# A two-layer hybrid block on one core: the 31-tap depthwise convolution as matmuls on four column tiles, and all low halves of the weights on VectorE

## The chip, the core and the metric

The kernel runs on one core of a Trainium2 chip. The metric is device time in microseconds (us) of one execution. The kernel before took 1141.38 us (median of 3 runs, 1138.75 to 1142.35). The names of the engines are those of the profile: PE is TensorE's matmul part and PEld its weight load, DVE is VectorE, ACT is ScalarE, POOL is GpSimd, SP is SyncE, which here only issues transfers. SPq is SP's queue of transfers, ACTq is ACT's.

## What is computed

Two layers, each on 256 tokens of width 1024, all in float32. A layer normalises its input, multiplies it with one wide matrix of 16,400 columns, sends pieces of the product through three branches (differential attention, a conformer convolution, a gated delta rule), gates the three results, adds them and multiplies once more. Cut to the branch that the change touches:

```python
def hybrid_layer(x, ...):
    h = rms_norm(x, norm_w)
    proj = h @ w_in                                   # (256, 16400)
    (aq, ak, av, az, c_glu, cz, dq, dk, dvv, dz, db, da, gate_logits) = jnp.split(proj, ...)
    y_a = diff_attention_branch(aq, ak, av, az, ...)  # 8 heads, ends in @ w_attn_out
    y_c = conformer_conv_branch(c_glu, cz, conv_dw_w, conv_dw_b, conv_ln_w, conv_ln_b, w_conv_out)
    y_d = gated_deltanet_branch(dq, dk, dvv, dz, ...) # 4-tap convs, chunked rule, @ w_dn_out
    g_a, g_c, g_d = jnp.split(jax.nn.sigmoid(gate_logits), 3, axis=-1)
    return x + (g_a * y_a + g_c * y_c + g_d * y_d) @ w_out

def conformer_conv_branch(glu_in, z, dw_w, dw_b, ln_w, ln_b, w_o):
    a, g = jnp.split(glu_in, 2, axis=-1)
    u = a * jax.nn.sigmoid(g)                         # (256, 1024)
    u = causal_depthwise_conv(u, dw_w) + dw_b         # 31 taps, each channel by itself
    u = layer_norm(u, ln_w, ln_b)
    u = jax.nn.silu(u) * jax.nn.silu(z)
    return u @ w_o

def causal_depthwise_conv(x, w):                      # w: (31, 1024); zeros stand before token 0
    return lax.conv_general_dilated(x, w[:, None, :], (1,), [(30, 0)],
                                    feature_group_count=1024, ...)
```

## The kernel before

**Weights.** The matrices of a layer are cut into 36 groups of 512 columns (the list `ORDER`), each group into four chunks of 256 rows by 512 columns: 144 chunks of 512 KB a layer, 288 in all. `load_chunk` (L297) handles one. SP's queue loads it into `w_raw` (L301). ACT rounds it to a format that TensorE takes in one pass, `w_hi` (L308). Then `w_lo = w_raw - w_hi` is made (L309) on DVE or on POOL, as a string of 144 digits says (`POOL`, L50). Each of the three tiles has three buffers: a load waits until an earlier `w_lo` has been made from its buffer, and a `w_hi` or `w_lo` waits until PE is done with an earlier chunk.

**Matmuls.** Activations are also kept as high and low half, so each product takes three matmuls (high by high, high by low, low by high). `group_a` (L360) makes the output with channels on partitions, by matmuls over 256 tokens; `group_b` (L323) with tokens on partitions, by matmuls over 512 columns. Both need some 24 times 256 columns a chunk. All other matmuls (the delta rule, attention, transposes) are plain float32 and run as two passes each; the trace has a record for each pass.

**Order.** PE's order is written out by hand. A layer goes through the steps of `SEQ` (L60): `v`, `k`, `q`, `w`, `a`, `z` each stand for groups of matmuls, `c0` and `c1` for the two halves of the conformer's input (L862), and then through gates and output matrices (`y_phase`, L1095). Between the k-steps of a group, `pump` (L266) runs a piece of a side stream (keys, queries and chunks of the delta rule, attention, the final layer norm), if its due time on a counted clock `clk` has come; each `mm` adds its cost in us to that clock. On the other engines a scheduler sets the order by priorities; `load_chunk` runs 340 ahead.

**The convolution.** `c_groups` leaves `u` as two tiles `c_u` of 128 partitions (channels) by 4 by 256 tokens (L877). The generator `conv_ops` (L887) then makes, for each of 8 channel tiles, one ACT instruction (last tap and bias, L891) and 30 instructions on DVE, `c_acc[sh:] += u[:256-sh] * w[30-sh]` (L894): 480 on DVE in the two layers. `filler` (L290) hands them out with the lowest priority at fourteen places of a layer (`CONV_PLAN`), from the second delta-rule value group to the attention output. `ln_stream` (L1151) reads the result `c_acc` late in the layer.

Of the kernel before, what the change touches and what calls it, by code (L numbers as in the profile page):

```python
# [10 lines left out]
F32 = mybir.dt.float32  # L11
# [47 lines left out]
W_AHEAD = 340  # L59
SEQ = "v0 k0 t0 v1 k1 c0 q0 w0 x0 q1 w1 x1 a0 c1 z0 z1 a1".split()  # L60
CONV_PLAN = {}
CONV_PLAN.update({("in", DV + GW): 36, ("in", AQ): 0, ("in", AK): 12, ("in", CA + GW): 32, ("in", DZ): 32, ("in", DZ + GW): 0, ("in", AQ + GW): 0, ("in", AK + GW): 20, ("dn", 0): 28, ("dn", GW): 8, ("in", AZ): 60, ("in", AZ + GW): 0, ("attn", 0): 12, ("attn", GW): 240})


PC_DW, PC_DB, PC_LW, PC_LB, PC_SC, PC_SUB, PC_DNW = 0, 248, 256, 264, 272, 368, 369
PC_N = 370
PR_AL, PR_DT, PR_LAM = 0, 8, 16
# [23 lines left out]
def kernel(  # L91
# [80 lines left out]
    with tc.issue_after(x_dma[-1].ins):  # L172
# [114 lines left out]
    counter = [0]  # L287
    conv = [None]

    def filler(key, ins):  # L290
        n = CONV_PLAN.get(key, 0)
        if n and ins is not None:
            with tc.high_priority(offset=-LOW), tc.issue_after(ins.ins):
                for _ in range(n):
                    next(conv[0], None)

    def load_chunk(l, g, c):  # L297
# [62 lines left out]
    def group_a(l, key, xs, evac, need=()):  # L360
# [3 lines left out]
        for c, (hi, lo) in enumerate(parts):  # L364
            for kk in range(KC):
# [80 lines left out]
    for l in range(DEPTH):  # L446
# [32 lines left out]
        def params():  # L479
# [382 lines left out]
        def c_groups(s):  # L862
# [19 lines left out]
            group_a(l, ("in", CG + s * GW), H, evac_g)  # L882
            group_a(l, ("in", CA + s * GW), H, evac_u)

        ac = act.tile([P, 8, T], F32, name="c_acc")

        def conv_ops():  # L887
            for ct in range(8):
                u = us[ct // 4][:, ct % 4, :]
                w0 = ct * 31  # L890
                S.activation(out=ac[:, ct, :], in_=u, func=AF.Identity,  # L891
                             scale=dww[:, w0 + 30:w0 + 31], bias=pc[:, PC_DB + ct:PC_DB + ct + 1])
                for sh in range(1, 31):
                    V.scalar_tensor_tensor(out=ac[:, ct, sh:T], in0=u[:, 0:T - sh],  # L894
                                           scalar=dww[:, w0 + 30 - sh:w0 + 31 - sh],
                                           in1=ac[:, ct, sh:T], op0=ALU.mult, op1=ALU.add)
# [435 lines left out]
```

## Time and profile before

| | before |
|---|---|
| median of 3 runs | 1141.38 us (1138.75 to 1142.35) |
| the profiled execution: its span, first to last instruction | 1144.1 us |
| mean granted clock of TensorE | 0.971 |
| busy: PE, DVE, ACT, POOL | 90%, 89%, 48%, 31% of the span |
| instructions in the trace | 17280, of them 6372 matmul passes |
| moved by DMA | 158.97 MB, mean 139 GB/s |

The profiled execution has no time of its own beside its span; the span is 2.7 us (0.2%) above the median of the runs. Busy shares of PE count from the start of a matmul to its modelled end, and neighbours overlap, so a PE that is busy isn't a PE at its peak. A row of a group of instructions gives their line in the kernel, the engine, the operation, what it writes and reads, how many there are, their busy time and mean duration, and how long the engine was idle before them and for whom. Windows are stretches of the span, in us from its start; an `x` and a number behind a busy time count instructions. The second layer repeats the first from about 558 us on.

### The profile page before, as it was taken

What the parts mean: (1) busy time and instruction counts of PE and PEld (TensorE: products, weight loads), DVE (VectorE), ACT (ScalarE), POOL (GpSimd) and SP (SyncE); (2) the same over time, 40 slices, a digit from 0 to 9 for tenths busy, and PEclk for the clock granted to TensorE, in tenths of its full rate; (3) what the DMA queues carried; (4) which work ended last, traced back from release to release, by engine and by line L of the source; (5) the groups of instructions that cost most, each with busy time, mean ns of one, the idle gap of its engine ahead of it and who ended that gap; (6) DMA issues with size and microseconds to landing.
All of it is one profiled execution on the core that took longest, in us unless ns stands there. A gap on an engine that the chain in (4) does not pass through costs nothing.

```text
span 1144.1 us, 17280 instructions
## 1 busy us (share of the span) xinstructions
PE 1034.5 (90%) x6372; PEld 901.7 (79%) x6372; DVE 1020.7 (89%) x1996; ACT 547.5 (48%) x995; POOL 359.0 (31%) x168
## 2 busy tenths in 40 slices
PE   7998989899998998898999889889999799899897
PEld 6897988897876876796889889879887678678775
DVE  5879898999998999988577989899999989998966
ACT  5734544344545553345466445443535455434543
POOL 2244132221162125425413332222113412253441
PEclk9999999999998999999999999998999899999998
DMA  6443333233344554454665433332433455545553
GB/s 211 149 127 111 129 125 115 93 111 96 109 129 140 160 178 139 153 173 149 189 208 164 129 116 125 120 102 93 129 111 111 129 157 173 150 152 163 158 172 109
DMA packets 46052, 158.97 MB, mean 139 GB/s; under 512 B 5392, under 2 KB 6416, under 8 KB 45968
## 3 DMA queue, kind: packets, MB, share of 16 engines
q1 hardware_dynamic: 42624, 153.11, 42.2%
q10 hardware_dynamic: 3312, 4.76, 1.3%
q8 instruction: 50, 0.82, 0.3%
q14 instruction: 34, 0.28, 0.1%
q0 software_dynamic: 32, 0.00, 0.1%
HBM read 155.75 MB, written 2.10 MB: 138 GB/s over the span
## 4 chain that ended last, share of the span: by engine, by line
DVE 51%; PE 34%; issue 7%; ACT 3%; DMA 2%; POOL 2%; SPq 0%; ACTq 0%; POOLq 0%; DVEq 0%
PE acc L245 26%; DVE c_acc L894 15%; DVE w_lo L309 10%; PE sg L245 4%; DVE wc L611 4%; DVE dn_t L702 2%; DMA w_raw<-in_wts 2%; ACT w_hi L308 2%; PE sg L249 1%; PE sa L249 1%; ACT a_pe L968 1%; DVE big L1065 1%; POOL w_lo L309 1%; DVE c_acc L1186 1%; PE sa L245 1%
## 5 line engine op out<-in xcount | busy, mean ns | idle before, releaser
L308 ACT CAST w_hi<-w_raw 128x1024 fp32r<-128x1024 f32 (+1 forms) x289 | 301.3, 1044 | 318.7 <-PE acc L245 186.0
L309 POOL TENSOR_TENSOR w_lo<-w_raw,w_hi 128x1024 fp32r<-128x1024 f32 x96 | 251.6, 2622 | 604.1 <-ACT w_hi L308 534.1
L309 DVE TENSOR_TENSOR w_lo<-w_raw,w_hi 128x1024 fp32r<-128x1024 f32 (+1 forms) x193 | 251.9, 1307 | 46.0 <-ACT w_hi L308 45.5
L894 DVE SCALAR_TENSOR_TENSOR c_acc<-c_u,pc,c_acc 128x245 f32<-128x245 f32 (+18 forms) x480 | 275.1, 608 | 2.3
L245 PE MATMUL acc<-h_hi,w_lo 128*128 128x256 f32 x768 | 222.1, 289 | 11.2 <-DVE w_lo L309 8.7
L245 PE MATMUL acc<-h_hi,w_hi 128*128 128x256 f32 x768 | 232.2, 302 | 0.0
L245 PE MATMUL acc<-w_lo,h_hi 128*128 128x512 f32 x512 | 204.5, 399 | 20.6 <-DVE w_lo L309 15.1
L245 PE MATMUL acc<-h_lo,w_hi 128*128 128x256 f32 x768 | 221.4, 288 | 0.0
L245 PE MATMUL acc<-w_hi,h_hi 128*128 128x512 f32 x512 | 212.4, 415 | 1.3 <-ACT w_hi L308 1.3
L245 PE MATMUL acc<-w_hi,h_lo 128*128 128x512 f32 x512 | 203.2, 397 | 0.0
L245 PEld LDWEIGHTS acc<-h_hi,w_lo 128*128 128x128 f32 x768 | 151.3, 197 | 12.4 <-DVE w_lo L309 9.5
L245 PEld LDWEIGHTS acc<-h_lo,w_hi 128*128 128x128 f32 x768 | 151.9, 198 | 0.7
L245 PEld LDWEIGHTS acc<-h_hi,w_hi 128*128 128x128 f32 x768 | 151.7, 198 | 0.5
L245 PEld LDWEIGHTS acc<-w_lo,h_hi 128*128 128x128 f32 x512 | 98.0, 191 | 44.3 <-DVE w_lo L309 20.9
L245 PEld LDWEIGHTS acc<-w_hi,h_lo 128*128 128x128 f32 x512 | 97.6, 191 | 20.9
L245 PEld LDWEIGHTS acc<-w_hi,h_hi 128*128 128x128 f32 x512 | 98.2, 192 | 18.8 <-ACT w_hi L308 2.1
L245 PE MATMUL acc<-w_lo,y_hi 128*128 128x512 f32 x192 | 77.5, 404 | 5.8 <-DVE w_lo L309 4.8
L611 DVE SCALAR_TENSOR_TENSOR wc<-wc,pc 128x255 f32<-128x255 f32 (+2 forms) x144 | 82.4, 608 | 0.3
L245 PE MATMUL acc<-w_hi,y_hi 128*128 128x512 f32 x192 | 78.2, 407 | 0.0
L245 PE MATMUL acc<-w_hi,y_lo 128*128 128x512 f32 x192 | 76.7, 399 | 0.1
L245 PEld LDWEIGHTS acc<-w_lo,y_hi 128*128 128x128 f32 x192 | 37.1, 193 | 17.2 <-DVE w_lo L309 7.9
L926 POOL TENSOR_TENSOR wa<-wa 128x512 f32<-128x512 f32 x16 | 23.7, 1478 | 70.4 <-DVE wa L924 64.3
(298 smaller groups left out, 1504.5 us busy)
## 6 DMA issues: line engine op xcount, KB each, us to landing
w_raw<-in_wts SPq DMA_DIRECT2D x288, 512.0 KB, 3.5
big<-in_x SPq DMA_DIRECT2D x4, 256.0 KB, 5.0
big<-in_x ACTq DMA_DIRECT2D x4, 256.0 KB, 4.6
x_keep<-big ACTq DMA_DIRECT2D x4, 256.0 KB, 4.3
vv<-in_fnw ACTq DMA_DIRECT2D x1, 512.0 KB, 4.9
big<-x_keep SPq DMA_DIRECT2D x2, 256.0 KB, 6.1
big<-x_keep ACTq DMA_DIRECT2D x2, 256.0 KB, 4.9
out<-c_u ACTq DMA_DIRECT2D x2, 256.0 KB, 2.0
```

The costliest lines, as they stand in the source:

```text
L245: TE.matmul(**kw)
L249: TE.transpose(out=out, in_=in_, identity=ident[0:n, 0:n])
L308: S.copy(out=hi[:, kk], in_=raw[:, kk])
L309: eng.tensor_sub(out=lo[:, kk], in0=raw[:, kk], in1=hi[:, kk].bitcast(F32))
L611: V.scalar_tensor_tensor(out=cv[:, i, s:T], in0=cs[:, i, 0:T - s], scalar=wts_[i][:, 3 - s:4 - s], in1=cv[:, i, s:T], op0=ALU.mult, op1=AL ...
L702: V.tensor_tensor(out=t1[:, :, 0:i + 1], in0=z[:, :, 0:i + 1], in1=nrep[:, 0:i + 1, :, i].rearrange("p j c -> p c j"), op=ALU.mult)
L894: V.scalar_tensor_tensor(out=ac[:, ct, sh:T], in0=u[:, 0:T - sh], scalar=dww[:, w0 + 30 - sh:w0 + 31 - sh], in1=ac[:, ct, sh:T], op0=ALU.m ...
L926: G.tensor_tensor(out=ra, in0=ra, in1=rb, op=ALU.add)
L968: S.activation(out=pe[:, m, :], in_=scs[m][:, ii, :], func=AF.Exp, bias=nmxs[m][:, ii:ii + 1], accum_out=sums[:, m:m + 1])
L1065: V.scalar_tensor_tensor(out=os_[:, h, :], in0=os_[:, h, :], scalar=rv[:, t, h:h + 1], in1=tzs[t][:, h, :], op0=ALU.mult, op1=ALU.mult)
L1186: V.tensor_scalar(out=pz[:, f, :], in0=pz[:, f, :], scalar1=ln4[:, ct:ct + 1], scalar2=ln4[:, 8 + ct:9 + ct], op0=ALU.mult, op1=ALU.add)
```

## The change

The convolution moves to PE. Its 31 taps, with a zero tap added, are cut into 8 groups `q` of 4. A tile `u4` holds, on its four blocks of 32 partitions, the same 32 channels at shifts 0, 1, 2 and 3 tokens; a tile `wd` holds diagonal 32x32 blocks of tap weights, one for each shift, channel block and `q`. One matmul of 128 rows by 32 columns adds four taps for 32 channels; four of them, one for each block `j` of 32 channels, go to the four blocks of 32 output partitions, and eight `q` finish 128 channels. `conv_group` has two such channel tiles, runs four times a layer (`d0`, `d1`, `d2` in `SEQ`, and once after the gates of the delta rule), and ACT takes the result from PSUM with bias and scale. That is 512 matmuls in plain float32 in the two layers.

`u4` needs `u` in another layout, so `c_groups` writes `u` to DRAM (`u_keep`, SP's queue), and `conv_load` reads it back in four transfers of 32 partitions, behind a load of 1 MB of `wd`. `u4` and `wd` have one buffer each. The `filler` and its plan are gone. The string `POOL` is all zeros: all 288 `w_lo` are made on DVE. A small load of positions moves from POOL's queue to ACT's.

```diff
-POOL = ("000001001001001000011010010001001001100101001001000110001010001010001101"
-        "101001001000100001001010001001001001001001010001001001001001001001001000")
+POOL = "0" * 144
-SEQ = "v0 k0 t0 v1 k1 c0 q0 w0 x0 q1 w1 x1 a0 c1 z0 z1 a1".split()
-CONV_PLAN = {}
-CONV_PLAN.update({("in", DV + GW): 36, ...})
+SEQ = "v0 k0 t0 v1 k1 c0 q0 w0 d0 x0 q1 w1 d1 x1 a0 c1 z0 z1 d2 a1".split()
+TAPQ = 8
+    u_keep = dram.tile([D, T], F32, name="u_keep")
+    u4 = const.tile([P, 8, T], F32, name="u4")
+    wd = const.tile([P, 2, TAPQ, 4, 32], F32, name="wd")
+        for i in range(1, 4):
+            G.memset(u4[32 * i:32 * i + 32, :, 0:i], 0.0)
-        nc.gpsimd.dma_start(out=pos_i, in_=positions.rearrange("b (c p) -> p (b c)", p=P))
+        nc.scalar.dma_start(out=pos_i, in_=positions.rearrange("b (c p) -> p (b c)", p=P))
...
             group_a(l, ("in", CG + s * GW), H, evac_g)
             group_a(l, ("in", CA + s * GW), H, evac_u)
+            nc.sync.dma_start(out=u_keep[s * GW:(s + 1) * GW].rearrange("(a p) t -> p a t", p=P), in_=us[s])
+            conv_load(2 * s)
 
         ac = act.tile([P, 8, T], F32, name="c_acc")
 
-        def conv_ops():
-            for ct in range(8):
-                u = us[ct // 4][:, ct % 4, :]
-                w0 = ct * 31
-                S.activation(out=ac[:, ct, :], in_=u, func=AF.Identity,
-                             scale=dww[:, w0 + 30:w0 + 31], bias=pc[:, PC_DB + ct:PC_DB + ct + 1])
-                for sh in range(1, 31):
-                    V.scalar_tensor_tensor(out=ac[:, ct, sh:T], in0=u[:, 0:T - sh],
-                                           scalar=dww[:, w0 + 30 - sh:w0 + 31 - sh],
-                                           in1=ac[:, ct, sh:T], op0=ALU.mult, op1=ALU.add)
-                    yield
+        def conv_load(n):
+            with tc.high_priority(offset=W_AHEAD):
+                nc.sync.dma_start(out=wd.rearrange("p f q j c -> p (f q j c)"), in_=cwd[l, n])
+                for i in range(4):
+                    nc.sync.dma_start(
+                        out=u4[32 * i:32 * i + 32, :, i:T],
+                        in_=u_keep[n * 2 * P:(n + 1) * 2 * P, 0:T - i].rearrange("(g c) t -> c g t", c=32))
+
+        def conv_group(n):
+            ps = acc_tile().rearrange("p (f t) -> p f t", f=2)
+            for f in range(2):
+                ct = 2 * n + f
+                for q in range(TAPQ):
+                    for j in range(4):
+                        mm((T - 4 * q) / 2400.0, out=ps[32 * j:32 * j + 32, f, 4 * q:T], lhsT=wd[:, f, q, j, :],
+                           rhs=u4[:, 4 * f + j, 0:T - 4 * q], start=(q == 0), stop=(q == TAPQ - 1))
+                S.activation(out=ac[:, ct, :], in_=ps[:, f, :], func=AF.Identity, scale=0.5,
+                             bias=pc[:, PC_DB + ct:PC_DB + ct + 1])
+                pump()
+            if n in (0, 2):
+                conv_load(n + 1)
...
         steps = {..., "d": conv_group}
...
         y_phase(GATE_D, "dn", (yd, list(enumerate(s_z))))
+        conv_group(3)
```

What the change does to the order shows at three places. The first is PE behind the step `w0` of the first layer (the first delta-rule value group, `group_a`; `t` is a tile of the delta rule's keys, transposed here). Before, the transposes are followed by further weight matmuls:

```order
L245 MATMUL acc<-h_lo,w_hi 128x256
L245 MATMUL acc<-h_hi,w_lo 128x256
L249 MATMUL sg<-cst,t_1251 128x128 x4
L245 MATMUL acc<-h_hi,w_hi 128x256
L245 MATMUL acc<-h_lo,w_hi 128x256
```

Now, with the step `d0` there (shown as `u_80` and `wd`; x4 are the four column tiles):

```order
L249 MATMUL acc<-h_lo,w_hi 128x256
L249 MATMUL acc<-h_hi,w_lo 128x256
L253 MATMUL sg<-cst,t_1256 128x128 x4
L249 MATMUL acc<-u_80,wd 32x256 x4
L249 MATMUL acc<-u_80,wd 32x252 x4
L249 MATMUL acc<-u_80,wd 32x248 x4
L249 MATMUL acc<-u_80,wd 32x244 x4
L249 MATMUL acc<-u_80,wd 32x240 x4
L249 MATMUL acc<-u_80,wd 32x236 x4
L249 MATMUL acc<-u_80,wd 32x232 x4
L249 MATMUL acc<-u_80,wd 32x228 x4
L249 MATMUL sg<-ones,gx 128x1 x8
```

Eight rows of four are one channel tile; one side stream's step stands between the two tiles of a group, and no weight matmul.

The second is DVE some way into the delta rule's first chunk (`gx` and `dn_r` are its tiles, L799 to L818; L920 and L924 are attention's rotary step). Before, runs of the convolution stand between the side streams and the `w_lo`:

```order
L818 TENSOR_TENSOR gx<-sg,dec 128x512
L309 TENSOR_TENSOR w_lo<-w_raw,w_hi 128x1024
L920 TENSOR_TENSOR wa<-acc,cosr 128x512
L924 TENSOR_TENSOR wa<-acc,sinr 128x8x32 x2
L894 SCALAR_TENSOR_TENSOR c_acc<-c_u,pc,c_acc 128x254 x2
L894 SCALAR_TENSOR_TENSOR c_acc<-c_u,pc,c_acc 128x253 x2
L894 SCALAR_TENSOR_TENSOR c_acc<-c_u,pc,c_acc 128x252 x2
L894 SCALAR_TENSOR_TENSOR c_acc<-c_u,pc,c_acc 128x251 x2
```

Now the same stretch has the `w_lo` and the side streams alone:

```order
L811 TENSOR_TENSOR gx<-sg,dec 128x512
L304 TENSOR_TENSOR w_lo<-w_raw,w_hi 128x1024
L923 TENSOR_TENSOR wa<-acc,cosr 128x512
L927 TENSOR_TENSOR wa<-acc,sinr 128x8x32 x2
L923 TENSOR_TENSOR wa<-acc,cosr 128x512
L792 SCALAR_TENSOR_TENSOR dn_r_2187<-sg,neg_eg,dn_r_2187 128x128 x4
L304 TENSOR_TENSOR w_lo<-w_raw,w_hi 128x1024
```

The convolution is gone from between them, and a `w_lo` comes after fewer other instructions.

The third is SP's queue from the start of the kernel. Before, it held the input and 85 chunks in a row; now:

```order
L884 DMA wd<-in_cwd 128x2048
L159 DMA big<-in_x 128x512 x2
L296 DMA w_raw<-in_wts 128x1024 x29
L877 DMA u_keep<-c_u 128x4x256
L296 DMA w_raw<-in_wts 128x1024
L886 DMA u_80<-u_keep 32x8x256
L886 DMA u_80<-u_keep 32x8x255
L886 DMA u_80<-u_keep 32x8x254
L886 DMA u_80<-u_keep 32x8x253
L296 DMA w_raw<-in_wts 128x1024 x8
L884 DMA wd<-in_cwd 128x2048
```

The first 1 MB of `wd` stands ahead of the input. The write of `u_keep` waits for DVE's last instruction on `u` (L877 of the kernel before), the first read of `u_keep` for the landing of that write, and the second `wd` for PE's last matmul of `d0`; the chunks stand behind each of these.

More of the change, by code (lines that the diff above doesn't have):

```diff
@@ L59 @@
 W_AHEAD = 340
-SEQ = "v0 k0 t0 v1 k1 c0 q0 w0 x0 q1 w1 x1 a0 c1 z0 z1 a1".split()
-CONV_PLAN = {}
-CONV_PLAN.update({("in", DV + GW): 36, ("in", AQ): 0, ("in", AK): 12, ("in", CA + GW): 32, ("in", DZ): 32, ("in", DZ + GW): 0, ("in", AQ + GW): 0, ("in", AK + GW): 20, ("dn", 0): 28, ("dn", GW): 8, ("in", AZ): 60, ("in", AZ + GW): 0, ("attn", 0): 12, ("attn", GW): 240})
-PC_DW, PC_DB, PC_LW, PC_LB, PC_SC, PC_SUB, PC_DNW = 0, 248, 256, 264, 272, 368, 369
-PC_N = 370
+SEQ = "v0 k0 t0 v1 k1 c0 q0 w0 d0 x0 q1 w1 d1 x1 a0 c1 z0 z1 d2 a1".split()
+TAPQ = 8
+PC_DB, PC_LW, PC_LB, PC_SC, PC_SUB, PC_DNW = 0, 8, 16, 24, 120, 121
+PC_N = 122
 PR_AL, PR_DT, PR_LAM = 0, 8, 16
@@ L97 @@
     wba: bass.AP,
+    cwd: bass.AP,
     pch: bass.AP,
@@ L287 @@
     counter = [0]
[L288 to L295, printed above, removed]
     def load_chunk(l, g, c):
@@ L332, in group_b @@
             if k == KT - 1:
-                filler(key, evac(ps))
+                evac(ps)
             pump()
@@ L382, in group_a @@
                 if k == KT - 1:
-                    filler(key, evac(ps))
+                    evac(ps)
                 pump()
@@ L459 @@
         scw = pc[:, PC_SC:PC_SC + 96]
-        dww = pc[:, PC_DW:PC_DW + 248]
         ln2 = lay.tile([P, 16], F32, name="ln2")
@@ L484, in params @@
                 masks()
-            V.tensor_scalar(out=dww, in0=dww, scalar1=0.5, scalar2=None, op0=ALU.mult)
             V.tensor_scalar(out=ln2, in0=pc[:, PC_LW:PC_LW + 16], scalar1=0.5, scalar2=None, op0=ALU.mult)
@@ L883, in c_groups @@
             group_a(l, ("in", CA + s * GW), H, evac_u)
+            nc.sync.dma_start(out=u_keep[s * GW:(s + 1) * GW].rearrange("(a p) t -> p a t", p=P), in_=us[s])
+            conv_load(2 * s)
         ac = act.tile([P, 8, T], F32, name="c_acc")
-        def conv_ops():
-            for ct in range(8):
-                u = us[ct // 4][:, ct % 4, :]
-                w0 = ct * 31
-                S.activation(out=ac[:, ct, :], in_=u, func=AF.Identity,
-                             scale=dww[:, w0 + 30:w0 + 31], bias=pc[:, PC_DB + ct:PC_DB + ct + 1])
-                for sh in range(1, 31):
-                    V.scalar_tensor_tensor(out=ac[:, ct, sh:T], in0=u[:, 0:T - sh],
-                                           scalar=dww[:, w0 + 30 - sh:w0 + 31 - sh],
-                                           in1=ac[:, ct, sh:T], op0=ALU.mult, op1=ALU.add)
-                    yield
-        conv[0] = conv_ops()
+        def conv_load(n):
[18 more added lines that the diff above has]
+                conv_load(n + 1)
         def q_group(hs):
@@ L1084 @@
         steps = {"v": v_group, "k": k_group, "c": c_groups, "q": q_group, "w": dv_group, "x": x_start,
-                 "a": qk_groups, "z": dz_group, "t": tables}
+                 "a": qk_groups, "z": dz_group, "t": tables, "d": conv_group}
         for step in SEQ:
@@ L1307 @@
     pch = np.concatenate(
-        [chan(a["conv_dw_w"], 8), chan(a["conv_dw_b"], 8), chan(a["conv_ln_w"], 8),
+        [chan(a["conv_dw_b"], 8), chan(a["conv_ln_w"], 8),
          chan(a["conv_ln_b"], 8), chan(a["dn_conv_w"], 24),
          chan(a["attn_subln_w"], 1), chan(a["dn_norm_w"], 1)], axis=2)
+    taps = np.zeros((DEPTH, 4 * TAPQ, D), np.float32)
+    taps[:, :31] = a["conv_dw_w"][:, ::-1]
+    taps = taps.reshape(DEPTH, TAPQ, 4, 4, 2, 4, 32)
+    cwd = np.zeros((DEPTH, 4, 4, 32, 2, TAPQ, 4, 32), np.float32)
+    for c in range(32):
+        cwd[:, :, :, c, :, :, :, c] = taps[..., c].transpose(0, 3, 2, 4, 1, 5)
+    cwd = cwd.reshape(DEPTH, 4, P, 2 * TAPQ * 4 * 32)
     prow = np.concatenate(
@@ L1316 @@
     arrays = {
-        "x": a["x"].reshape(T, D), "positions": a["positions"], "wts": wts, "wba": wba,
+        "x": a["x"].reshape(T, D), "positions": a["positions"], "wts": wts, "wba": wba, "cwd": cwd,
         "pch": pch, "prow": prow,
@@ L1320 @@
     }
-    nc = _bacc.Bacc("TRN2", target_bir_lowering=False, num_devices=1)
+    nc = _bacc.Bacc("TRN2", target_bir_lowering=False, num_devices=1, dynamic_dma_scratch_size=1024)
     aps, feed = [], {}
```

## Prediction

> **What bounds the kernel now.** I read the page first, then stretches of the span by stage, then the paces of PE's matmuls, then the groups on DVE and POOL.
>
> The page, busy shares and the chain of waits that ended last:
>
> ```profile
> span 1144.1 us, 17280 instructions
> PE 1034.5 (90%) x6372; PEld 901.7 (79%) x6372; DVE 1020.7 (89%) x1996; ACT 547.5 (48%) x995; POOL 359.0 (31%) x168
> ...
> DVE 51%; PE 34%; issue 7%; ACT 3%; DMA 2%; POOL 2%; SPq 0%; ACTq 0%; POOLq 0%; DVEq 0%
> PE acc L245 26%; DVE c_acc L894 15%; DVE w_lo L309 10%; PE sg L245 4%; DVE wc L611 4%; DVE dn_t L702 2%; DMA w_raw<-in_wts 2%; ACT w_hi L308 2%; PE sg L249 1%; PE sa L249 1%; ACT a_pe L968 1%; DVE big L1065 1%; POOL w_lo L309 1%; DVE c_acc L1186 1%; PE sa L245 1%
> ```
>
> PE and DVE are both near 90%, and the chain runs over DVE more than over PE; the convolution (L894) alone is 15% of it. So taking work from DVE can pay, but only down to what PE needs by itself. How much is that? First the stages: the two layers before the convolution starts (25 to 195, 583 to 754), while it runs (195 to 480, 754 to 1040), and after it.
>
> ```profile
> core 0: us, PE busy (x) PEld busy (x) DVE busy (x) ACT busy (x) POOL busy (x), PEclk, DMA share, GB/s
> 0.00:25.00 25.00, 17.77 (x68) 13.88 (x69) 13.36 (x27) 13.71 (x26) 4.94 (x7) 1.00 0.66 215
> 25.00:195.00 170.00, 152.48 (x1218) 145.60 (x1218) 147.81 (x329) 84.29 (x140) 53.32 (x27) 0.96 0.40 128
> 195.00:480.00 285.00, 258.66 (x1408) 215.33 (x1407) 275.32 (x555) 129.87 (x275) 83.24 (x35) 0.96 0.41 128
> 480.00:583.00 103.00, 97.64 (x524) 83.30 (x524) 79.67 (x94) 53.34 (x72) 40.06 (x19) 0.99 0.57 182
> 583.00:754.00 171.00, 157.96 (x1258) 150.34 (x1257) 148.22 (x325) 86.12 (x142) 53.33 (x27) 0.98 0.43 136
> 754.00:1040.00 286.00, 259.67 (x1428) 217.07 (x1427) 276.62 (x560) 131.00 (x276) 83.75 (x35) 0.97 0.41 131
> 1040.00:1144.10 104.10, 90.29 (x479) 76.17 (x477) 79.66 (x111) 49.22 (x67) 40.34 (x19) 0.97 0.47 152
> ```
>
> While the convolution runs, DVE is busy 275 of 285 us and PE idles 26 a layer; before that, DVE is busy 148 of 170 without any convolution. The granted clock is below 1 in the same stretches: 4% of 170 us is 7 us lost, 4% of 285 is 11. Idle time and lost clock together make 41 us in the two early stages (17.5, 13.0, 6.8, 3.4), 73 in the two middle ones (26.3, 26.3, 11.4, 8.6), 12 late (without the tail) and 2.5 at the start.
>
> Those are lower bounds, since a PE in a gap counts as busy to the modelled end of its last matmul. So I also go by PE's paces, from the chain and the timeline (start, length, what, how many):
>
> ```profile
> 1040.73 17.16 PE acc L245 x143
> ...
> 180.60 1.39 PE acc L245 x6
> ...
> 4.70 0.47 PE L249 MATMUL sa<-cst,big 128*128 128x128 f32 x1 [4.70 <-DMA cst<-in_consts]
> ...
> 367.53 1.05 PE L245 MATMUL sg<-big,a_at 128*128 128x128 f32 x8
> 368.34 0.47 PE L245 MATMUL acc<-w_hi,y_hi 128*128 128x512 f32 x1
> ...
> 1135.21 0.39 PE L245 MATMUL acc<-w_hi,c_acc 128*128 128x512 f32 x1
> ```
>
> Unhindered, a 256-column matmul of the weight groups takes 17.16/143 = 0.120 us, a 512-column one 1.39/6 = 0.232, a float32 pass of 128 columns (368.34 - 367.53)/8 = 0.10. A chunk is 24 of the first kind (96 chunks) or 12 of the second (192): 276 + 535 = 811 us. The other 6372 - 4608 = 1764 passes would be 178 us at 0.10; some are much shorter, and I take 150. So PE needs 961 us, and 183 are lost, 4.7 before its first matmul and 8.5 after its last. The 170 between are 1.33 times the 128 above; split in the same ratio: **early 54, middle 97, late 16, start 3**.
>
> **What goes from DVE.**
>
> ```profile
> L309 POOL TENSOR_TENSOR w_lo<-w_raw,w_hi 128x1024 fp32r<-128x1024 f32 x96 | 251.6, 2622 | 604.1 <-ACT w_hi L308 534.1
> L894 DVE SCALAR_TENSOR_TENSOR c_acc<-c_u,pc,c_acc 128x245 f32<-128x245 f32 (+18 forms) x480 | 275.1, 608 | 2.3
> ...
> L309 DVE TENSOR_TENSOR w_lo<-w_raw,w_hi x193: 685/1217/3743, 9.3 to 1128.6; 128x1024 fp32r<-128x1024 f32 x191, 128x512 fp32r<-128x512 f32 x2
> ...
> L894 DVE SCALAR_TENSOR_TENSOR c_acc<-c_u,pc,c_acc x480: 431/461/2656, 196.5 to 1037.8; 128x249 f32<-128x249 f32 x14, 128x246 f32<-128x246 f32 x10, 128x243 f32<-128x243 f32 x10, 128x237 f32<-128x237 f32 x10
> ```
>
> (The last two rows give minimum, median and maximum in ns.) The convolution leaves 275.1 us. The 96 `w_lo` from POOL come in at the median of 1.217 us: 117. DVE is then busy 1020.7 - 275.1 + 117 = 863 us, 75% of the old span. It should be less: the convolution's instructions have a median of 461 ns, a mean of 608 and a maximum of 2656, about the length of one `w_lo` on POOL (2622). I read that as DVE standing still while POOL's instruction runs. If so, a `w_lo` on POOL cost DVE about what it costs to make it there, and the early stages, which have POOL's `w_lo` and no convolution, lose nothing by the swap. `w_lo` also comes 1.4 us sooner after `w_hi`.
>
> In the middle stage POOL is busy 83 us, 252/359 of it by `w_lo`: 22 of them at 2.622. DVE falls there from 275 to 275 - 138 + 27 = 164 of 285 us: 58%. I take 70 of the 97 lost there as won. Early, DVE is at 87% and stays near it; what helps is that `d0` and `d1`, PE work without new `w_lo`, stand in that stage and let DVE catch up. I take 24 of 54. Late, the layer norm's chain on DVE stays: 4 of 16. **Won: 98.** Between ends: 40, if most gaps are chains of dependent steps that a freer DVE doesn't shorten, and 130.
>
> **What comes to PE.** 512 float32 matmuls, two passes each, of 256 down to 228 columns, 242 in the mean. A pass over the whole array, and passes on two row halves (attention's scores, L951, four matmuls with the halves alternating):
>
> ```profile
> 502.73 0.59 PE L245 MATMUL sa<-gx,ones 128*128 128x256 f32 x2
> ...
> L245 PE MATMUL sa<-gx,ones x8: 377/377/378, 483.6 to 1059.5; 128*128 128x256 f32 x8
> ...
> 358.88 1.13 PE L245 MATMUL sa<-t,t 64*128 64x256 f32 x8
> 359.95 0.39 PE L245 MATMUL sa<-mask_at,identb 128*128 128x256 bf16 x2
> ...
> 358.90:359.18 0.28, 0.28 (x2) 0.28 (x4) 0.00 (x0) 0.00 (x0) 1.00 0.83 337
> ```
>
> On the whole array the second pass starts 0.59 - 0.377 = 0.213 us after the first, so 242 columns take 0.201. On row halves, eight passes took 359.95 - 358.88 = 1.07 us, not 8 x 0.213 = 1.70, and in the first 0.28 us two were on their way. So tiles of the array do run at once: four slots of 0.213 and 0.22 for getting in and out. Column tiles don't occur in this trace. Bounds: 1024 x 0.201 = 206 us one after another, a fourth of it, 52, if four run at once; the nearest row, the row halves, reached its full factor, so I take 52. Sixteen stretches with 0.22 each add 3: **55**. The upper end is 209. ACT's part is the same as before (16 instructions for 16).
>
> [...]
>
> **What comes to the queues.**
>
> ```profile
> SPq L301 <- DVE w_lo L309: 431.2, 135, 7.7
> SPq L301 <- POOL w_lo L309: 361.6, 93, 8.4
> ...
> w_raw<-in_wts SPq DMA_DIRECT2D x288, 512.0 KB, 3.5
> ...
> x_keep<-big ACTq DMA_DIRECT2D x4, 256.0 KB, 4.3
> ...
> 6.25 0.90 PE L249 MATMUL sa<-cst,big 128*128 128x128 f32 x3 [1.08 <-DMA big<-in_x]
> ```
>
> At the start, 1.05 MB of `wd` stand ahead of the input that PE waits for at 6.25. At the 215 GB/s of the first window that is 4.9 us, at its full share (215/0.66) 3.2: **4**. Each layer has two round trips of `u` through DRAM: the write lands after some 4.3 us, then 1 MB of `u4` takes 3.2 to 4.9, and chunks stand behind both. Cover: SP waits for free buffers 431 + 362 us in all, so loads are early; up to five chunks (14 us of PE) lie ahead. Without that cover a trip costs 9 us; four cost 0 to 36, and I take **4**. The waits of `wd` for PE's `d0` hold chunks only while PE runs `d0` itself. In all, 8 x (1.05 + 1.04) + 2.1 = 19 MB are added to 159, no bound.
>
> **Sum**, on the profiled execution: 1144 - 98 + 55 + 4 + 4 = 1109. The median of the runs is 0.2% below that span, so **1106 us** for the runs.
>
> **Rivals** (times of the span, less 3 for the runs).
> - *Only two passes run at once* (0.13): a tile's second pass goes before the next tile's first, or its weight load lies open, so the gain is a half. The convolution is 103 + 3; more PE work also fills gaps, so won 106: 1144 - 106 + 106 + 8 = 1152, **1149**. For it: the eight passes on row halves would also take 1.07 us as five slots in strict order. Against: two at once from the first slot.
> - *No overlap* (0.08): 209, won 115: 1144 - 115 + 209 + 8 = 1246, **1243**. For it: no row shows column tiles. Against: nothing but the row halves.
> - *The gaps stay* (0.14): PE's waits are chains PE, ACT, DVE, PE, in which each step's own length counts and not DVE's load. The lower end of 40 is won, and 15 more because a quarter of PE's new work falls into the gaps: 1144 - 55 + 63 = 1152, **1149**. For it: the early stages idle with DVE at 87%. Against: 15% of the chain lies in L894 itself. It decides if less than 63 is won.
> - *Weights come late* (0.08), the slower side: SP's queue waits for `u_keep` with chunks behind it, and eight loads of 2 MB push chunks back by 6 us each; 48 us more and the rest as forecast: **1150**. It decides once the lead is under 9 us.
>
> **How the numbers follow.** The forecast has 0.57, with its own range 1080 to 1138 (won 130 to 66). The range 1077 to 1162 takes in the rivals but the one without overlap, and leaves out about 0.2. A measurement here tells no change within 0.3%, 3.4 us. Faster: 0.55 of the forecast, 0.04 of the gaps that stay, 0.03 of two at once, 0.01 of late weights: 0.63. Same: 0.01, 0.03, 0.02, 0.01: 0.07. Slower: the remaining 0.30.
>
> **What would show it.** Right: the passes that read `wd` start four at a time, a stretch of 64 takes about 3.5 us; DVE's busy time is near 800 with no `w_lo` or tap above 2 us while POOL works; PE idles under 10 us a layer in the middle, with a clock nearer 1. Wrong: a stretch of 7 or 13 us; gaps in the middle that still end on DVE with DVE free before; `w_hi` waiting for `w_raw` behind `u4`.

## The result and the profile after

The changed kernel takes **1107.8 us** (median of 4 runs, 1104.5 to 1110.0) against 1140.4 (4 runs) for the kernel before: a ratio of 0.9707, 95% interval 0.9678 to 0.9736. 1106 was forecast.

The page of the changed kernel (span, busy times, the chain of waits, the groups of `w_lo` and of the convolution on PE):

```profile
span 1108.2 us, 18945 instructions
PE 1061.9 (96%) x7396; PEld 920.1 (83%) x7396; DVE 805.4 (73%) x1610; ACT 550.3 (50%) x995; POOL 108.0 (10%) x74
...
PE 78%; DVE 14%; ACT 2%; issue 2%; POOL 1%; DMA 1%; ACTq 0%; DVEq 0%
...
L304 DVE TENSOR_TENSOR w_lo<-w_raw,w_hi 128x1024 fp32r<-128x1024 f32 (+1 forms) x289 | 361.0, 1250 | 165.9 <-ACT w_hi L303 164.4
...
L249 PE MATMUL acc<-u,wd 128*32 128x256 f32 (+7 forms) x1024 | 55.6, 369 | 0.5 <-ACT c_acc L898 0.5
```

The chain now runs over PE for 78% of the span (34% before) and over DVE for 14% (51%). DVE gave up 215 us. POOL is down from 359 to 108 us. The convolution's matmuls keep PE busy for 55.6 us, overlaps counted once.

The same stretches of time as before (columns: us, then busy us and instructions of each engine, the granted clock, the DMA share, GB/s):

```profile
25.00:195.00 170.00, 162.89 (x1492) 150.29 (x1491) 141.84 (x346) 87.46 (x145) 16.30 (x12) 1.00 0.50 158
195.00:480.00 285.00, 281.92 (x1834) 238.88 (x1833) 192.78 (x362) 140.93 (x288) 21.48 (x13) 1.00 0.51 162
480.00:583.00 103.00, 100.60 (x508) 84.73 (x508) 77.30 (x129) 56.08 (x81) 13.68 (x8) 0.97 0.57 181
583.00:754.00 171.00, 164.11 (x1455) 150.76 (x1453) 137.85 (x307) 80.17 (x135) 19.73 (x14) 0.97 0.47 145
754.00:1040.00 286.00, 283.53 (x1827) 240.39 (x1828) 197.63 (x371) 144.25 (x285) 19.58 (x12) 1.00 0.53 164
1040.00:1108.00 68.00, 57.04 (x244) 45.84 (x242) 47.26 (x75) 30.56 (x43) 13.07 (x8) 0.90 0.40 133
```

In the two middle stretches PE idles 3.1 and 2.5 us (26.3 and 26.3 before), at a clock of 1.00 (0.96 and 0.97). The early ones go from 17.5 and 13.0 us idle to 7.1 and 6.9. DVE is busy 193 and 198 us there (164 forecast). In the main this looks as forecast. The experiments show that the reasons were only half right.

### The profile page after: what moved, and what is told of

Its sections match the earlier page's. It is cut to its first block, busy times and chain, and to the rows that moved or that the text cites. A ratio compares the mean times of both kernels' runs of the same rounds, so it can differ in the third digit from the quotient of the medians.

```text
span 1108.2 us, 18945 instructions
## 1 busy us (share of the span) xinstructions
PE 1061.9 (96%) x7396; PEld 920.1 (83%) x7396; DVE 805.4 (73%) x1610; ACT 550.3 (50%) x995; POOL 108.0 (10%) x74
## 4 chain that ended last, share of the span: by engine, by line
PE 78%; DVE 14%; ACT 2%; issue 2%; POOL 1%; DMA 1%; ACTq 0%; DVEq 0%
PE acc L249 64%; PE sg L249 9%; DVE w_lo L304 4%; PE sg L253 2%; PE sa L249 2%; DVE wc L604 2%; PE sa L253 1%; ACT w_hi L303 1%; DVE dn_t L695 1%; POOL gf L645 1%; DVE c_acc L1190 1%; DMA cst<-in_consts 1%; DVE dn_z L697 1%; POOL c_acc L1196 0%; DMA pr<-in_prow 0%
## 5 line engine op out<-in xcount | busy, mean ns | idle before, releaser
L304 DVE TENSOR_TENSOR w_lo<-w_raw,w_hi 128x1024 fp32r<-128x1024 f32 (+1 forms) x289 | 361.0, 1250 | 165.9 <-ACT w_hi L303 164.4
L249 PE MATMUL acc<-h_hi,w_hi 128*128 128x256 f32 x768 | 227.9, 297 | 1.8 <-ACT w_hi L303 1.8
L249 PE MATMUL acc<-w_lo,h_hi 128*128 128x512 f32 x512 | 200.2, 391 | 2.1 <-DVE w_lo L304 2.1
L249 PEld LDWEIGHTS acc<-h_hi,w_lo 128*128 128x128 f32 x768 | 147.9, 193 | 5.7 <-DVE w_lo L304 5.7
L249 PEld LDWEIGHTS acc<-h_hi,w_hi 128*128 128x128 f32 x768 | 148.1, 193 | 2.5 <-ACT w_hi L303 2.0
L249 PEld LDWEIGHTS acc<-h_lo,w_hi 128*128 128x128 f32 x768 | 148.2, 193 | 0.6
L604 DVE SCALAR_TENSOR_TENSOR wc<-wc,pc 128x255 f32<-128x255 f32 (+1 forms) x144 | 65.9, 498 | 0.0
L249 PE MATMUL acc<-u,wd 128*32 128x256 f32 (+7 forms) x1024 | 55.6, 369 | 0.5 <-ACT c_acc L898 0.5
L1117 POOL TENSOR_TENSOR big<-big,wc 128x512 f32<-128x512 f32 x16 | 28.2, 1786 | 281.8 <-DVE wc L1114 281.8
L929 POOL TENSOR_TENSOR wa<-wa 128x512 f32<-128x512 f32 x16 | 26.3, 1650 | 259.8 <-DVE wa L927 219.1
L249 PEld LDWEIGHTS acc<-u,wd 128*32 128x32 f32 x1024 | 31.6, 110 | 20.3 <-issue 1.8
```

The source lines that it names most:

```text
L249: TE.matmul(**kw)
L304: eng.tensor_sub(out=lo[:, kk], in0=raw[:, kk], in1=hi[:, kk].bitcast(F32))
L604: V.scalar_tensor_tensor(out=cv[:, i, s:T], in0=cs[:, i, 0:T - s], scalar=wts_[i][:, 3 - s:4 - s], in1=cv[:, i, s:T], op0=ALU.mult, op1=AL ...
L929: G.tensor_tensor(out=ra, in0=ra, in1=rb, op=ALU.add)
L1117: G.tensor_tensor(out=ms, in0=ms, in1=gts[i][t], op=ALU.add)
```

## The experiments

At first the theory is the prediction's: VectorE's convolution was the load that made TensorE wait, and the place of `w_lo` hardly matters. What took its place after the first runs is in the later expectations, each with its rival. Times are medians; ratios are to the kernel before, timed on the same chip beside each, with 95% intervals.

### The two halves of the change apart

The changed kernel with the old digits back (a third of the `w_lo` on POOL again):

```diff
-POOL = "0" * 144
+POOL = ("0000010010010010000110100100010010011001010010010001...")
```

> The changed kernel with the old string of digits: the convolution stays on PE, and 96 of the 288 low halves go back to POOL. Theory (an instruction on POOL holds DVE while it lasts, so POOL takes nothing off DVE): DVE has slack now, but these 96 low halves come 1.4 us later and hold DVE for up to 2.6 us each; 1110 to 1130, with DVE's mean for a low half and for the short convolution's taps back above their medians. Rival (POOL relieves DVE, the all-zero string is a cost that the freer DVE merely hides): 1095 to 1107, with DVE's busy time about 100 us lower than the changed kernel's 805.

And the kernel before with the zeros alone, the convolution still on DVE:

```diff
-POOL = ("0000010010010010000110100100010010011001010010010001...")
+POOL = "0" * 144
```

> The kernel before with all 288 low halves on DVE, the convolution still on DVE. Theory (same as for the run with the old string): the 117 us that come to DVE are about what the holds cost it, so 1130 to 1160, DVE's busy time 1000 to 1060, and no tap above 1 us. Rival (POOL relieves DVE): DVE's busy time grows by 117 to about 1137, which is the whole old span; 1200 to 1260.

| convolution on | `w_lo` on POOL: 96 | none |
|---|---|---|
| DVE | 1142.4 (kernel before) | **1084.5** (0.9497, 0.9471 to 0.9522) |
| PE | 1129.5 (0.9893, 0.9869 to 0.9918) | 1107.8 (0.9707, 0.9678 to 0.9736) |

The first run ended in the theory's range, the second missed both expectations, by more than 45 us. The zeros alone win 58 us; the convolution's move alone wins 13 (1.1%). Behind the zeros the move does not help: it costs 23. Pages of the run with the old digits back and of the run with zeros alone, the second first:

```profile
span 1081.0 us, 17318 instructions
PE 1009.3 (93%) x6372; PEld 887.9 (82%) x6372; DVE 974.1 (90%) x2092; ACT 554.1 (51%) x997; POOL 102.7 (10%) x72
```

```profile
span 1127.8 us, 18922 instructions
PE 1063.1 (94%) x7396; PEld 920.7 (82%) x7396; DVE 776.4 (69%) x1514; ACT 548.4 (49%) x995; POOL 342.1 (30%) x170
```

With zeros alone DVE does 96 more instructions than before (2092 for 1996) and is busy 47 us less (974.1 for 1020.7). So each `w_lo` on POOL had cost DVE 1.22 us and 47/96 = 0.49 more, some 1.7 us, where making it on DVE takes 1.22. The rows of one line on DVE (the delta rule's short convolution, both inputs in SBUF; minimum, median and maximum in ns) show where that time was, in the run with the digits back and in the one with zeros alone:

```profile
L605 DVE SCALAR_TENSOR_TENSOR wc<-wc,pc x144: 468/476/2618, 48.6 to 743.2; 128x255 f32<-128x255 f32 x48, 128x254 f32<-128x254 f32 x48, 128x253 f32<-128x253 f32 x48
```

```profile
L610 DVE SCALAR_TENSOR_TENSOR wc<-wc,pc x144: 466/476/484, 46.4 to 708.0; 128x255 f32<-128x255 f32 x48, 128x254 f32<-128x254 f32 x48, 128x253 f32<-128x253 f32 x48
```

The same 144 instructions reach 2618 ns, about the length of one `w_lo` on POOL (2622), or never pass 484.

With the convolution on PE it is otherwise. There the zeros raise DVE's busy time, from 776.4 to 805.4: each `w_lo` on POOL had cost DVE some 1.22 - 29/96 = 0.92 us, less than making it there, and the zeros still win 22 us. DVE's sum cannot explain that gain. What falls with it are PE's waits for `w_lo` (with the digits back, then in the changed kernel) and the waits of `w_hi` for `w_raw`, 28.0 us there and 0.3 in the changed kernel:

```profile
PE acc L250 <- DVE w_lo L305: 17.2, 11, 2.3
PE acc L250 <- POOL w_lo L305: 6.2, 5, 1.7
```

```profile
PE acc L249 <- DVE w_lo L304: 6.6, 7, 2.1
```

How the 22 us divide between the two was not tried.

### Is it POOL that holds VectorE, or a late `w_lo`?

Zeros alone still doesn't say which: a `w_lo` on POOL takes 2.6 us, holds its `w_raw` longer, and may hold DVE. So idle instructions came back to POOL, behind a `w_lo` that DVE had already made:

```diff
-POOL = ("0000010010010010000110100100010010011001010010010001...")
+POOL = "0" * 144
+HOLD = (the old digits)
...
                 eng.tensor_sub(out=lo[:, kk], in0=raw[:, kk], in1=hi[:, kk].bitcast(F32))
+            if hold:
+                G.tensor_sub(out=raw, in0=raw, in1=hi.bitcast(F32))
```

> The kernel before, with all w_lo made on VectorE (as in the run with the zeros alone, 1084), and at the places of the old digits GpSimd then does an instruction of the same size and length whose result nobody reads (raw minus w_hi, in place, after VectorE has read both). The output stays the same. Theory: an instruction of GpSimd with two inputs holds VectorE while it runs, so taking w_lo away from GpSimd freed VectorE's time. Then the idle instructions bring the loss back: DVE busy 1060 to 1150 in the place of 974, taps up to 2.3 us and more, 1125 to 1175 us. Rival: w_lo on GpSimd was only late for its matmuls (2.6 us in the place of 1.2) and VectorE is not held. Then w_lo is as early as in the run with zeros and the time stays at 1080 to 1092, with taps at 460 ns and w_lo at 1.2 us.

Measured: **1240.0** (1.0845, 1.0811 to 1.0878), far above the rival and above the theory too. These instructions hold `w_raw` as well as, perhaps, DVE, so a second run took them off the weights' buffers (`spare` is a tile of its own):

```diff
+            if hold:
+                for kk in range(KC):
+                    G.tensor_sub(out=spare, in0=hi[:, kk].bitcast(F32), in1=hi[:, kk].bitcast(F32))
```

> The kernel before with zeros for the digits, and idle instructions on GpSimd as in the run that came to 1240 us, but apart from the weights' buffers: two subtractions of half the size read w_hi and write a spare tile, so w_raw is released as early as with zeros alone. It divides the 156 us which the idle instructions cost (1240 - 1084) between VectorE held by GpSimd and w_raw released late (w_hi waited 119 us for w_raw in that run). Theory: VectorE is held, by some 1.7 us for each idle pair (DVE's busy time rose by 160 us for 96): DVE is busy 1090 to 1150 us and the time is 1160 to 1240. Rival: the late release did it; DVE stays under 1020 and the time under 1110.

Measured: **1198.6** (1.0495, 1.0461 to 1.0530), inside the theory's range, the rival out. The pages, the run with `w_raw` first:

```profile
PE 1059.5 (85%) x6372; PEld 916.2 (74%) x6372; DVE 1134.0 (91%) x2092; ACT 553.3 (45%) x997; POOL 348.8 (28%) x168
```

```profile
PE 1047.5 (88%) x6372; PEld 908.8 (76%) x6372; DVE 1094.6 (91%) x2092; ACT 554.4 (46%) x997; POOL 370.1 (31%) x264
```

DVE runs the same 2092 instructions as with zeros alone, and is busy 160 us longer (1.67 for each idle instruction of 2.53 us) and 120 us longer (1.26 for each pair, of 1.40 us each; 1.7 was expected). The time rises by 156 and by 114, in both runs about as much as DVE's busy time. Whether the 41 us between the two runs come from `w_raw`, released late (`w_hi` waits for it 119.4 us in the first, 57.1 in the second, 4.9 with zeros alone), or from DVE, held 40 us less, is not divided. A stretch of the first run's timeline (start, length, what), then two such instructions of the run with zeros alone:

```profile
63.97 2.95 DVE L615 SCALAR_TENSOR_TENSOR wc<-wc,pc 128x253 f32<-128x253 f32 x2
...
64.12 2.52 POOL L313 TENSOR_TENSOR w_raw<-w_raw,w_hi 128x1024 f32<-128x1024 f32 x1 [7.62 <-DVE w_lo L311]
```

```profile
49.81 0.87 DVE L610 SCALAR_TENSOR_TENSOR wc<-wc,pc 128x253 f32<-128x253 f32 x2
```

Two instructions that take 0.87 us take 2.95 when POOL starts during the first: the second ends just behind POOL's.

POOL can also be the one that is held. In the kernel before, two of its 96 `w_lo` take 6.9 us. One of them, and the taps and the `w_lo` on DVE inside it:

```profile
1003.23 4.31 DVE L894 SCALAR_TENSOR_TENSOR c_acc<-c_u,pc,c_acc 128x243 f32<-128x243 f32 x11
1004.01 6.87 POOL L309 TENSOR_TENSOR w_lo<-w_raw,w_hi 128x1024 fp32r<-128x1024 f32 x1 [9.70 <-ACT w_hi L308]
1007.46 1.22 DVE L309 TENSOR_TENSOR w_lo<-w_raw,w_hi 128x1024 fp32r<-128x1024 f32 x1
```

There DVE's instructions keep their own length (1.22 us for the `w_lo`), and POOL's becomes longer by 4.5 us (6.87 against its median of 2.41), about the 4.7 that they take inside it (1004.01 to 1008.68).


### What the convolution costs on TensorE

The changed kernel without convolution (ACT copies `u` to `c_acc`):

```diff
-                for q in range(TAPQ):
-                    for j in range(4):
-                        mm((T - 4 * q) / 2400.0, out=ps[32 * j:32 * j + 32, f, 4 * q:T], lhsT=wd[:, f, q, j, :],
-                           rhs=u4[:, 4 * f + j, 0:T - 4 * q], start=(q == 0), stop=(q == TAPQ - 1))
-                S.activation(out=ac[:, ct, :], in_=ps[:, f, :], func=AF.Identity, scale=0.5,
+                S.activation(out=ac[:, ct, :], in_=us[ct // 4][:, ct % 4, :], func=AF.Identity, scale=0.5,
```

> The changed kernel without the convolution: no matmuls of it, no loads of wd and u4, no round trip of u; ACT writes c_acc from u itself, and the clock that places the side streams counts as before. Theory (PE is the bound, and the 55 us of convolution matmuls add to it in full): 1107.8 - 55 - 7 at the start - 2 for the queue = 1040 to 1050. Rival (half of the convolution's matmuls stand in gaps of PE that are there anyhow, most of all early in a layer): 1065 to 1080, with PE idling longer where d0 and d1 stood.

Measured: 1059.1 (0.9275, 0.9237 to 0.9313), between the two expectations. With no `w_lo` on POOL, the convolution therefore costs 49 us on PE, its loads among them, and, in its old place, 25 on DVE.

Then the order of its matmuls: all tap groups of one column tile before the next tile, and two tiles in turn:

```diff
-                for q in range(TAPQ):
-                    for j in range(4):
+                for j in range(4):
+                    for q in range(TAPQ):
```

> The changed kernel, with the matmuls of the convolution in another order: all eight tap groups of one column tile, then those of the next, in the place of the four tiles in turn. The same matmuls, the same result. Theory: the four column tiles run at once only because neighbours in the order lie on different tiles; 16 stretches of 64 passes take 13 us each in the place of 3.5, and the time goes from 1108 to 1240 to 1262 us. Rival: matmuls of 32 columns are short of themselves (a quarter of the array costs a quarter), the order doesn't matter: 1105 to 1115, a stretch at 3.5 us.

```diff
-                for q in range(TAPQ):
-                    for j in range(4):
+                for jp in (0, 2):
+                  for q in range(TAPQ):
+                    for j in (jp, jp + 1):
```

> The changed kernel, with the convolution's column tiles taken in pairs: two tiles in turn through all tap groups, then the other two. Theory: as many passes run at once as different column tiles stand next to each other, so a stretch of 64 takes 6.8 us, and 16 of them put 16 x 3.3 = 53 us on 1108: 1155 to 1165 us. Rival: two tiles are enough to hide what hides (the pass of one beside the weight load of the other), 3.5 to 4.5 us a stretch: 1106 to 1125.

One stretch of 64 passes (the second channel tile of the first group) in the timelines of the changed kernel, of two tiles and of one:

```profile
141.91 3.47 PE L249 MATMUL acc<-u,wd 128*32 128x256 f32 x64
```

```profile
147.25 5.99 PE L249 MATMUL acc<-u,wd 128*32 128x256 f32 x64
```

```profile
149.22 11.01 PE L249 MATMUL acc<-u,wd 128*32 128x256 f32 x64
```

One tile at a time took 1229.0 us (1.076, 1.073 to 1.0791), two 1147.5 (1.0048, 1.0023 to 1.0074). Both lie 8 to 11 us below what the theory had, since its stretches of 13 and 6.8 us were too long. Sixteen stretches at 11.01 - 3.47 make 120.6 us, and 1229.0 - 1107.8 = 121.2; at 5.99 - 3.47 they make 40.3, measured 39.7. The order alone does it, and in the changed kernel what PE takes longer goes into the time one to one.

### The start and the queue

The first `wd` behind the 19th chunk, and the positions behind the constants on ACT's queue:

```diff
-        nc.scalar.dma_start(out=pos_i, in_=positions.rearrange("b (c p) -> p (b c)", p=P))
+        with tc.issue_after(cst_ins.ins):
+            nc.scalar.dma_start(out=pos_i, in_=positions.rearrange("b (c p) -> p (b c)", p=P))
...
+            if counter[0] == 18:
+                with tc.issue_after(w_ins.ins):
+                    nc.sync.dma_start(out=wd.rearrange("p f q j c -> p (f q j c)"), in_=cwd[0, 0])
```

> The changed kernel with the first 1 MB of wd loaded behind the 19th chunk instead of ahead of the input, and the load of the positions behind the constants. Theory (the start lost 7 to 8 us: 3.5 for the input behind 1 MB, and the rest because the first chunk waits for a semaphore that an earlier transfer holds): 1098 to 1102, with the first chunk issued near 1.7 us and the first weight matmul near 9.3. Rival (only the megabyte counts, and the late first chunk is covered): 1103 to 1105.

The first matmul of the changed kernel, then of this one:

```profile
8.27 0.47 PE L253 MATMUL sa<-cst,big 128*128 128x128 f32 x1 [8.27 <-DMA cst<-in_consts]
```

```profile
4.24 0.47 PE L254 MATMUL sa<-cst,big 128*128 128x128 f32 x1 [4.24 <-DMA cst<-in_consts]
```

PE starts 4.0 us sooner, the first `w_hi` even 5.1 (7.5 for 12.6 us). But the 25th chunk's `w_hi` is only 0.6 us ahead, the 49th's 0.9 behind, and the time is 1109.8 (0.9716, 0.9690 to 0.9743), the same as 1107.8. Both expectations missed: the start is worth nothing here. The lead is lost between 25 and 195 us, where PE idles 11.1 us for 7.1 and the granted clock is 0.98 for 1.00, an estimated 3.4 us (2% of 170). Why is not shown.

For the round trips of `u`, the loads of `wd` and `u4` were made once only, with the same matmuls on whatever then stands there:

```diff
-            nc.sync.dma_start(out=u_keep[s * GW:(s + 1) * GW].rearrange("(a p) t -> p a t", p=P), in_=us[s])
-            conv_load(2 * s)
+            if l == 0 and s == 0:
+                nc.sync.dma_start(out=u_keep[s * GW:(s + 1) * GW].rearrange("(a p) t -> p a t", p=P), in_=us[s])
+                conv_load(2 * s)
...
-            if n in (0, 2):
-                conv_load(n + 1)
```

> The changed kernel, in which wd and u4 are loaded once, at the start of the first layer, and u goes to DRAM only there: 16 MB of loads and three writes fall out, the matmuls are the same, but most of the convolution is made of the wrong channels (its output is not the reference's). It prices what the prediction put at 4 us for the round trips of u through the queue. Theory (the chunks ahead cover them): 1102 to 1108 us. Rival (chunks behind the loads come late): under 1098, and waits of w_hi for w_raw that the changed kernel has and this one has not.

Measured: 1101.8 (0.9644, 0.9627 to 0.9660): 6 us below the changed kernel, 0.25 below the theory's range. No wait of `w_hi` for `w_raw` is behind it (0.3 us in both kernels), as the rival would have it. By the starts of the `w_hi` the difference lies in the second layer. There the granted clock differs. The two profiled executions, the changed kernel first:

```profile
core 0: 1108.2 us, clock 0.986
```

```profile
core 0: 1100.4 us, clock 0.993
```

By these means the clock takes an estimated 15.5 us of the first (1.4% of 1108.2) and 7.7 of the second (0.7% of 1100.4), which is as much as the whole difference between the two. All four runs with the loads made once had 0.993; of the changed kernel's four runs two had 0.993 and 0.995, and they took 1105.5 and 1104.5 us, 3 to 4 above 1101.8. So the queue costs 3 to 4 us at a like clock and 6 by the medians. Whether the loads are what lowers the clock in the other runs is open.

### A better place for the convolution

With zeros alone, one wait of PE stands out, that of the layer norm's mean for `gx`, behind the last taps on DVE:

```profile
PE sa L244 <- DVE gx L1157: 22.5, 2, 11.3
```

Two ways to end it. A quarter of the convolution (channel tiles 6 and 7) on PE, behind the delta rule's gates:

```diff
-            for ct in range(8):
+            for ct in range(6):
...
         y_phase(GATE_D, "dn", (yd, list(enumerate(s_z))))
+        conv_group(3)
```

> The kernel before with zeros for the digits (1084), and a quarter of the convolution, the channel tiles 6 and 7, moved to TensorE's column tiles behind the delta rule's gates; the other six tiles stay on VectorE. Theory: what is left to win in the run with zeros is the tail of the convolution on VectorE, for which the layer norm's mean waits 11.5 us in each layer: VectorE gives up 69 us, TensorE takes 13 and loses no waits elsewhere: 1070 to 1080 us. Rival: VectorE's other chains (w_lo, the delta rule) fill what is freed and the 13 us on TensorE are simply added: 1084 to 1098 us.

Or the taps handed out earlier, all still on DVE:

```diff
-CONV_PLAN.update({("in", DV + GW): 36, ..., ("attn", 0): 12, ("attn", GW): 240})
+CONV_PLAN.update({("in", DV + GW): 60, ("in", AK): 60, ("in", CA + GW): 60, ("in", DZ): 60})
```

> The kernel before with zeros for the digits (1084), and the convolution on VectorE given out earlier, 60 taps at each of four weight groups, in the place of 14 entries with a tail at attention's last. Nothing is moved between engines. Theory: the layer norm's mean waits 11.5 us a layer because the last taps come late; earlier taps end that wait: 1062 to 1078 us. Rival: VectorE is full there (274 of 285 us), so earlier taps only push its other work back, and what the mean gains is lost by w_lo and the delta rule's steps: 1084 us or more.

The first took 1074.8 (0.9413, 0.9377 to 0.9448), and the wait is gone from PE's list. The second took 1078.7 (0.9448, 0.9415 to 0.9481), just outside its range, and its mean still waits:

```profile
PE sa L244 <- DVE gx L1157: 17.2, 2, 8.6
```

Earlier taps gain 6 us though DVE is full there. That what stays is DVE's sum was not tested by itself. Both were then put together, with one tile in eight on PE, and the start mended as above:

```diff
-            for ct in range(8):
+            for ct in range(7):
...
-            for f in range(2):
+            for f in (1,):
...
+CONV_PLAN.update({("in", DV + GW): 60, ("in", AK): 60, ("in", CA + GW): 60, ("in", DZ): 30})
...
         y_phase(GATE_D, "dn", (yd, list(enumerate(s_z))))
+        conv_group(3)
```

> A version that puts together what the runs showed: the kernel before with zeros for the digits; seven channel tiles of the convolution stay on VectorE, their taps given out earlier (60 at each of three weight groups, 30 at a fourth); tile 7 alone runs on TensorE's column tiles behind the delta rule's gates; wd behind the 19th chunk, the positions behind the constants. Theory: against the hybrid with two tiles on TensorE (1075) TensorE saves 2 x 6.5 us, and VectorE's 14 us more a layer fit, since with no tile moved the mean waited 8.6 us: 1060 to 1068 us. Rival: with the mean's wait gone the chunks' w_lo and attention's steps on VectorE set the pace, and the 13 us come back as waits: 1071 to 1080 us.

Measured: **1061.4** (0.9301, 0.9271 to 0.9331), 46 us below the changed kernel and 13 below the hybrid; what the start and the earlier taps have in it was not divided. Its page, and the first of PE's waits:

```profile
span 1056.8 us, 17527 instructions
PE 1012.1 (96%) x6500; PEld 888.0 (84%) x6500; DVE 943.9 (89%) x2032; ACT 551.0 (52%) x995; POOL 103.8 (10%) x74
...
PE sa L256 <- DVE y_lo L411: 5.9, 2, 2.9
PE sg L256 <- DVE a_pe L1010: 5.0, 6, 1.3
PE sa L256 <- DMA cst<-in_consts: 4.0, 1, 4.0
```

No wait of PE in the list is over 5.9 us in sum, and the time is within the spread of the kernel without any convolution (1055.7 to 1062.4). DVE is as full as before the change (89%), and PE is at 96%: a share near 90% is by itself no sign that DVE is the bound.

## Why the prediction came out right, and where its reasons were wrong

**Conv on PE, 55: right, by two errors.** The group is 55.6 us. But one after another the passes take 11.01/64 = 0.172 us, not 0.201, so the upper end was 176 and not 206; and four at once are 11.01/3.47 = 3.17 times as fast, not four times. Two at once are 1.84 times. That only two run at once in the order of the change, as the first rival's 103 us have it, was the author's estimate, which no run shows: there it is four. The rivals with two passes at once and without overlap are out: their orders were run, and show what they would have cost (40 and 121 us more). One bound doesn't come out of its terms: 130 won makes 1144 - 130 + 63 - 3 = 1074, not 1080.

**Won 98: right in size, in part by luck.** By the prediction's own count PE needs 961 + 55 = 1016 us in a span of 1108.2, so 92 are lost, 8.3 of them before the first matmul and 8.8 behind the last: 75 between, where 170 were. 95 won. The middle stage went as forecast (idle and lost clock 73 before, 5.6 now: 67 won, 70 forecast). The early stages won 22 of 41 and the late one nothing. That the sum came within 2 us of the measured time is more than its reasons carry, as the next step shows.

**The step that failed is the swap of `w_lo`, costed at nothing.** "A `w_lo` on POOL cost DVE about what it costs to make it there, and the early stages lose nothing by the swap." The reading beneath it, DVE standing still while POOL's instruction runs, was right (two instructions of 0.87 us took 2.95 beside POOL's 2.52). Its price was not worked out: the runs give some 1.7 us of DVE for each at DVE's old load, against 1.22 (and 0.92 with the convolution on PE). The swap also ends most waits of `w_hi` for `w_raw` (71.2 us before, 4.9 with zeros alone). It is worth 58 us alone and 22 behind the convolution's move. And 98 was put down to DVE's lighter load, with a price of 55 + 4 + 4 for the convolution on PE; the runs give this second half a gain of 13 us alone and a loss of 23 behind the swap. In the early stages, too, it was not `d0` and `d1` alone: with zeros alone, PE's idle time falls in the same stretches of time (each stage comes somewhat sooner there):

```profile
25.00:195.00 170.00, 160.38 (x1304) 151.88 (x1302) 152.78 (x367) 94.22 (x156) 19.23 (x14) 1.00 0.44 137
195.00:480.00 285.00, 267.25 (x1555) 229.37 (x1554) 274.18 (x594) 140.12 (x279) 15.66 (x11) 0.98 0.47 145
```

In the first layer that is 9.6 us early for 17.5, at a clock of 1.00 for 0.96. In the middle 17.8 us stay idle, with DVE still at 274 of 285 us. That part the convolution's move does win. But it costs 49 us in all on PE.

**The gaps stay (0.14): wrong.** Counted as above, the lost time is 183 before, 112 (digits back), 120 (zeros alone), 92 (both): either half alone wins more than this rival's 55. With the digits back POOL does nearly what it did before, and DVE is busy 244 us less. The two halves remove much of the same waits, so their gains don't add: 71 + 63 would be 134, and 91 came.

**Start 4 and queue 4.** The first matmul came 3.6 us later, as forecast, but an earlier one brings nothing. The queue costs 3 to 6. **Weights come late (0.08): wrong**: `w_hi` waits 0.3 us for `w_raw` (71.2 before).

**What would show it.** A stretch of 64 in 3.47 us (3.5 forecast), DVE at 805 (near 800), PE idle 3 us a layer in the middle (under 10), the clock at 1.00: right. "No `w_lo` above 2 us while POOL works" was wrong: three of the 289 are longer, and each lies beside another instruction of POOL.

```profile
L304 DVE TENSOR_TENSOR w_lo<-w_raw,w_hi x289: 678/1225/2861, 13.3 to 1092.4; 128x1024 fp32r<-128x1024 f32 x144, 128x512 fp32r<-128x512 f32 x1
```

## What to carry to other kernels

When a change has two halves, price each half alone before adding them: a sum of the right size can hide that one half pays for the other. Work given to POOL to relieve DVE is to be charged with the time DVE stands while it runs (here an estimated 1.7 us an instruction with DVE 89% busy, and 0.92 with DVE at 69%, from DVE's busy times with and without it); here the sign was in the maxima of DVE's own groups, which came up to the length of POOL's instruction (2618 ns beside 2622). And of the work that is moved from a full engine to the one that ends the chain, move only as much as ends the wait that shows in the list: here an eighth of the convolution, with the other taps handed out earlier, was enough, and moving all of it cost more than it won.

## What the runs showed of the hardware

- While POOL subtracted one SBUF tile from another, DVE's instructions with two SBUF inputs could be held until it ended: those of the short convolution took up to 2618 ns for a median of 476 with the digits back, at most 484 with zeros alone, and 96 idle instructions of 2.5 us brought 160 us of DVE's busy time. Twice in the kernel before it was POOL that was held (6.9 us for a median of 2.41). Instructions of DVE with an input in PSUM ran on in the line that was compared: in the kernel before, eight of its sixteen lie wholly inside a `w_lo` on POOL, and with 676 to 685 ns none is longer than the rest by more than 3 ns:

```profile
L1111 DVE SCALAR_TENSOR_TENSOR wc<-wc,acc x16: 676/680/685, 450.5 to 1113.4; 128x512 f32<-128x512 f32 x16
```

- Four column tiles that share all rows ran float32 passes at once when they alternated in the order: a stretch of 64 took 3.47 us (0.054 a pass), against 5.99 in pairs and 11.01 (0.172 a pass) one after another. So the order of the four mattered here.
- The granted clock of the profiled execution was 0.971 in the kernel before, with PE busy 90% of the span, and 0.986 in the changed kernel, with 96%; in the two runs with idle instructions on POOL it was 0.941 with 85% and 0.951 with 88%, and with the old digits back 0.989 with 94%. Whether PE's gaps set it was not tried by itself, and runs of one kernel differ: 0.986 to 0.995 in the four of the changed kernel.
